# A batched 64x64 matrix product on one Trainium2 core: the preparation of the next tile is put ahead of this tile's matmuls, and b is cast on another engine

## The chip, the cores and the metric

The kernel runs on 1 core of a Trainium2 chip. The time is the device time in microseconds (us) of one execution. A profile of one execution stands beside the times; its span runs from the first to the last instruction of the program, and that execution's own time is a little longer than its span. The engines are called as in the profile: PE is TensorE (PEld its weight loads), DVE is VectorE, ACT is ScalarE, POOL is GpSimd and SP is SyncE. POOL and SP here mostly issue DMAs.

## The reference

1024 independent products of 64x64 matrices, float32 in and out:

```
a: (1024, 64, 64) float32, b: (1024, 64, 64) float32
out = np.matmul(a, b).astype(np.float32)
```

a and b are 16.78 MB each, and so is the output.

## The kernel before

The batch is cut into 16 tiles of 64 products. A tile is 16 groups (g) of 4 products (h). For each tile t:

- **Load.** Four DMAs on POOL's queue (one for each h, L59) bring a into `a_sb`, each 256 KB of float32 that the DMA turns into 128 KB of bfloat16. One DMA on SP's queue (L63) brings 1 MB of b into `b_sb`, as float32. There are four buffers of each, and the loop calls `load(t + 3)` at the head of round t. POOL's DMAs use eight completion semaphores in turn, so a DMA on POOL's queue is not issued before the DMA eight places earlier has landed; a load also waits until the copy out of the buffer that it takes (L80 for a, L103 for b) is done.
- **Prepare.** DVE copies a into `a_bf` (L80), so that the four products of a group stand side by side. PE transposes it in 16 pieces of 128x128 into two PSUM tiles `at_ps` (L88). DVE and ACT copy one half each of every `at_ps` to `at_sb` (L95, L97; for each `at_ps` ACT's copy waits for DVE's). DVE then writes four diagonal blocks of 32 partitions into `at_bd` (L101): the weights of a matmul that does four products at once. The rest of `at_bd` was zeroed at the start (L70); there are two such buffers. DVE also casts b to bfloat16, into `b_bf` (L103).
- **Multiply.** 64 matmuls of 128x128 weights by 128x64 (L111), in four quarters of 16 that go to a PSUM tile `o_ps` each. ACT copies each quarter to `o_sb` (L120); there are three `o_sb` buffers, so the first of these copies for tile t also waits until the store of tile t-3 has landed.
- **Store.** One DMA of 1 MB on POOL's queue (L122), behind the loads of a that were put there earlier.

Each engine works through a fixed list. The list is not in the order of the Python text: when the program is built, a scheduler orders the instructions of each engine, and it has put the 16 tiles in pairs (both tiles are prepared, then both are multiplied, then both are stored). In the names below the number behind `a_sb`, `at_sb` or `o_sb` tells the tiles apart.

Of the kernel before, what the change touches and what calls it, by code (L numbers as in the profile page):

```python
# [1 line left out]

# [5 lines left out]

fp32 = mybir.dt.float32
bf16 = mybir.dt.bfloat16  # L10


@with_exitstack
def kernel(
    ctx: ExitStack,
    tc: tile.TileContext,
    a: bass.AP,
    b: bass.AP,
    out: bass.AP,
):  # L20

    nc = tc.nc
    B, M, K = a.shape
    _, _, N = b.shape
    assert (M, K, N) == (64, 64, 64) and B % 64 == 0

    T = 64
    n_t = B // T
    AHEAD = 3

    a_v = a.rearrange("(t g h) (mp v) k -> t h g mp (v k)", h=4, g=16, v=8)
    b_v = b.rearrange("(t g h) (kp u) n -> t (h kp) g (u n)", h=4, g=16, u=2)
    o_v = out.rearrange("(t g h) (mo w) n -> t (h mo) g (w n)", h=4, g=16, w=2)

    consts = ctx.enter_context(tc.tile_pool(name="consts", bufs=1))
    a_pool = ctx.enter_context(tc.tile_pool(name="a_pool", bufs=AHEAD + 1))  # L40
    b_pool = ctx.enter_context(tc.tile_pool(name="b_pool", bufs=AHEAD + 1))
    work = ctx.enter_context(tc.tile_pool(name="work", bufs=2))
    o_pool = ctx.enter_context(tc.tile_pool(name="o_pool", bufs=3))
    t_psum = ctx.enter_context(
        tc.tile_pool(name="t_psum", bufs=4, space=bass.MemoryType.PSUM)
    )
    o_psum = ctx.enter_context(
        tc.tile_pool(name="o_psum", bufs=4, space=bass.MemoryType.PSUM)
    )

    bd_tiles = [
        consts.tile([128, 64, 4, 32], bf16, name=f"at_bd{i}") for i in range(2)
    ]
    a_tiles, b_tiles = {}, {}

    def load(t):
        a_sb = a_pool.tile([128, 4, 8, 64], bf16, name="a_sb")
        for h in range(4):
            nc.gpsimd.dma_start(  # L59
                out=a_sb[:, h, :, :].rearrange("p v k -> p (v k)"), in_=a_v[t, h]  # L60
            )
        b_sb = b_pool.tile([128, 16, 128], fp32, name="b_sb")
        nc.sync.dma_start(out=b_sb[:], in_=b_v[t])  # L63
        a_tiles[t], b_tiles[t] = a_sb, b_sb

    load(0)
    identity = consts.tile([128, 128], bf16)
    make_identity(nc, identity)
    for bd in bd_tiles:
        nc.vector.memset(bd[:], 0.0)  # L70
    for t in range(1, AHEAD):
        load(t)

    for t in range(n_t):
        if t + AHEAD < n_t:
            load(t + AHEAD)
        a_sb, b_sb, at_bd = a_tiles.pop(t), b_tiles.pop(t), bd_tiles[t % 2]

        a_bf = work.tile([128, 8, 4, 64], bf16, name="a_bf")
        nc.vector.tensor_copy(a_bf[:], a_sb[:].rearrange("p h v k -> p v h k"))  # L80
        a_cols = a_bf[:].rearrange("p v h k -> p v (h k)")

        at_sb = work.tile([128, 2, 2, 128, 4], bf16, name="at_sb")
        for w in range(2):
            at_ps = t_psum.tile([128, 4, 2, 128], bf16, name="at_ps")
            for vo in range(4):
                for u in range(2):
                    nc.tensor.transpose(  # L88
                        at_ps[:, vo, u, :], a_cols[:, 2 * vo + w, u::2], identity[:]
                    )  # L90
            for u in range(2):
                dst = at_sb[:, w, u, :, :]
                src = at_ps[:, :, u, :].rearrange("p vo q -> p q vo")
                if u == 0:
                    nc.vector.tensor_copy(dst, src)  # L95
                else:
                    nc.scalar.copy(dst, src)  # L97
        at_v = at_sb[:].rearrange("p w u (g mp) vo -> p (w u g) (mp vo)", g=16)
        for h in range(4):
            rows = slice(32 * h, 32 * h + 32)  # L100
            nc.vector.tensor_copy(at_bd[rows, :, h, :], at_v[rows, :, :])  # L101
        b_bf = work.tile([128, 16, 128], bf16, name="b_bf")
        nc.vector.tensor_copy(b_bf[:], b_sb[:])  # L103
        o_sb = o_pool.tile([128, 4, 4, 2, 64], fp32, name="o_sb")
        for gq in range(4):
            o_ps = o_psum.tile([128, 4, 2, 64], fp32, name="o_ps")
            for g4 in range(4):
                g = 4 * gq + g4
                for w in range(2):
                    for u in range(2):  # L110
                        nc.tensor.matmul(  # L111
                            o_ps[:, g4, w, :],
                            at_bd[:, (2 * w + u) * 16 + g, :, :].rearrange(
                                "p h mo -> p (h mo)"
                            ),
                            b_bf[:, g, 64 * u : 64 * u + 64],
                            start=(u == 0),
                            stop=(u == 1),
                        )
            nc.scalar.copy(o_sb[:, gq, :, :, :], o_ps[:])  # L120

        nc.gpsimd.dma_start(  # L122
            out=o_v[t], in_=o_sb[:].rearrange("p q g w n -> p (q g w n)")
        )


# [1 line left out]
_INS = ['a', 'b']  # L128
_OUTS = [((1024, 64, 64), 'float32')]


# [23 lines left out]
```

## Time and profile before

| | us |
|---|---|
| median of 3 runs | 151.15 (151.05 to 152.82) |
| the profiled execution's own time | 150.8 |
| its span | 148.9 |

| engine | busy us | share of the span |
|---|---|---|
| PE | 64.4 | 43% |
| DVE | 104.9 | 70% |
| ACT | 53.5 | 36% |
| POOL (mostly issuing DMAs) | 62.6 | 42% |

A share of busy time is a mean over the whole span. The span has a stretch in which loads, work and stores run side by side and a tail in which only work and stores are left, and the two have to be read apart. A row of the timeline gives the start, the duration, the engine, the line and the operation, and in brackets how long the engine had been idle and what ended that. "Landing" is the time from the issue of a DMA until its completion is seen. In the view by stretches of time, the row of each stretch ends with the clock that PE was granted (1.00 is full speed), the mean busy share of the 16 DMA engines (a little over 1 where packets overlap) and the GB/s that they moved; of a this counts the bfloat16 side, half of what is read.

### The profile page before, as it was taken

The numbers are of one execution on the slowest core, as the hardware profiler recorded it, in microseconds if no ns is written. First come the engines' busy times: TensorE is split into PE (matmuls) and PEld (weight loads), VectorE is DVE, ScalarE is ACT, GpSimd is POOL, SyncE is SP. The second block draws the span as 40 slices with busy tenths as digits, with TensorE's granted clock in tenths as the row PEclk, the third lists the DMA queues.
The fourth block names the chain that finished last, engine by engine and source line by source line (L and its number), as shares of the span: only waits on it lengthen the run. The fifth ranks groups of instructions, "written<-read, shape, count | busy, mean of one in ns | idle before, by whom it ended". The sixth has DMA issues, their size and how long they took to land.

```text
span 148.9 us, 3081 instructions
## 1 busy us (share of the span) xinstructions
PE 64.4 (43%) x1280; PEld 62.0 (42%) x1280; DVE 104.9 (70%) x130; ACT 53.5 (36%) x97; POOL 62.6 (42%) x86
## 2 busy tenths in 40 slices
PE   0005225960893058500990079402990059429400
PEld 0004215950893058500890078302880059429400
DVE  5754499799978297938995498919985497994000
ACT  3000052763320914064502733082602827616500
POOL 7644364336622165712983174614754303300410
PEclk9999999998569758955598557965599556975865
DMA  3999999999999999999999999999999995892594
GB/s 77 292 290 292 291 293 293 295 286 276 293 364 383 322 291 275 370 308 290 283 348 366 309 292 287 368 310 291 294 321 369 195 356 207 237 273 68 169 265 129
DMA packets 22031, 42.15 MB, mean 283 GB/s; under 512 B 1537, under 2 KB 9729, under 8 KB 22017
## 3 DMA queue, kind: packets, MB, share of 16 engines
q0 software_dynamic: 13568, 25.17, 66.7%
q1 hardware_dynamic: 8448, 16.78, 33.2%
q8 instruction: 10, 0.16, 0.4%
q14 instruction: 5, 0.03, 0.1%
HBM read 33.55 MB, written 16.78 MB: 338 GB/s over the span
## 4 chain that ended last, share of the span: by engine, by line
DMA 52%; issue 19%; POOL 11%; DVE 5%; PE 4%; ACT 3%; POOLq 1%; ACTq 0%; DVEq 0%
DMA a_sb<-in_a_dram 44%; POOL out_dram L122 8%; DMA out_dram<-o_sb 8%; PE o_ps L111 4%; POOL a_sb L59 2%; DVE at_sb L95 2%; DVE at_bd L101 2%; ACT at_sb L97 2%; ACT o_sb L120 1%; POOLq L150 1%; DVE b_bf L103 1%; DVE a_bf L80 0%; POOL identity masks.py:199 0%; POOL identity masks.py:197 0%; POOLq L122 0%
## 5 line engine op out<-in xcount | busy, mean ns | idle before, releaser
L111 PE MATMUL o_ps<-b_bf,at_bd 128*128 128x64 bf16 x1024 | 48.1, 225 | 59.3 <-DVE at_bd L101 59.3
L111 PEld LDWEIGHTS <-at_bd 128*128 128x128 bf16 x1024 | 46.6, 120 | 61.3 <-DVE at_bd L101 61.3
L59 POOL DMA_DIRECT2D a_sb<-in_a_dram x64 | 41.4, 652 | 50.8 <-DMA a_sb<-in_a_dram 23.7
L101 DVE COPY at_bd<-at_sb 32x2048 bf16<-32x2048 bf16 x64 | 49.7, 776 | 17.5 <-ACT at_sb L97 16.6
L120 ACT COPY o_sb<-o_ps 128x512 f32<-128x512 f32 x64 | 35.6, 591 | 65.7 <-PE o_ps L111 33.5
L122 POOL DMA_DIRECT2D out_dram<-o_sb x16 | 20.6, 1290 | 28.2 <-ACT o_sb L120 21.9
L97 ACT COPY at_sb<-at_ps 128x512 bf16<-128x512 bf16 x32 | 17.4, 624 | 20.2 <-DVE at_sb L95 20.0
L88 PE MATMUL at_ps<-identity,a_bf 128*128 128x128 bf16 x256 | 17.4, 231 | 15.8 <-DVE a_bf L80 15.8
L88 PEld LDWEIGHTS <-a_bf 128*128 128x128 bf16 x256 | 15.9, 104 | 16.1 <-DVE a_bf L80 16.1
L103 DVE CAST b_bf<-b_sb 128x2048 bf16<-128x2048 f32 x16 | 19.3, 1226 | 2.2 <-PE o_ps L111 2.2
L95 DVE COPY at_sb<-at_ps 128x512 bf16<-128x512 bf16 x32 | 19.9, 680 | 0.0
L80 DVE COPY a_bf<-a_sb 128x2048 bf16<-128x2048 bf16 x16 | 10.8, 694 | 8.7 <-DMA a_sb<-in_a_dram 7.7
L70 DVE MEMSET at_bd<- 128x4096 uint32 x2 | 6.9, 3472 | 2.5 <-PEq L139 1.7
L97 ACT ACT_TABLE_LOAD x1 | 1.3, 1283 | 0.7 <-PEq L139 0.7
masks.py:199 POOL TENSOR_SCALAR_AFFINE_SELECT identity<-identity 128x128 bf16<-128x128 bf16 x1 | 0.4, 364 | 0.0
masks.py:197 POOL MEMSET identity<- 128x128 bf16 x1 | 0.3, 266 | 0.0
L139 POOL MEMSET const-float32-0.0<- 128x1 f32 x1 | 0.1, 98 | 0.2 <-issue 0.2
L139 POOL MEMSET const-bfloat16-1.0<- 128x1 bf16 x1 | 0.1, 101 | 0.0
L139 POOL MEMSET const-uint8-127<- 128x1 uint8 x1 | 0.1, 101 | 0.0
L139 POOL MEMSET const-float32-1.0<- 128x1 f32 x1 | 0.1, 98 | 0.0
## 6 DMA issues: line engine op xcount, KB each, us to landing
out_dram<-o_sb POOLq DMA_DIRECT2D x16, 1024.0 KB, 10.9
a_sb<-in_a_dram POOLq DMA_DIRECT2D x64, 128.0 KB, 11.7
b_sb<-in_b_dram SPq DMA_DIRECT2D x16, 0.5 KB, 14.8
```

The source lines that it names most:

```text
L59: nc.gpsimd.dma_start(out=a_sb[:, h, :, :].rearrange("p v k -> p (v k)"), in_=a_v[t, h])
L70: nc.vector.memset(bd[:], 0.0)
L80: nc.vector.tensor_copy(a_bf[:], a_sb[:].rearrange("p h v k -> p v h k"))
L88: nc.tensor.transpose(at_ps[:, vo, u, :], a_cols[:, 2 * vo + w, u::2], identity[:])
L95: nc.vector.tensor_copy(dst, src)
L97: nc.scalar.copy(dst, src)
L101: nc.vector.tensor_copy(at_bd[rows, :, h, :], at_v[rows, :, :])
L103: nc.vector.tensor_copy(b_bf[:], b_sb[:])
L111: nc.tensor.matmul(o_ps[:, g4, w, :], at_bd[:, (2 * w + u) * 16 + g, :, :].rearrange("p h mo -> p (h mo)"), b_bf[:, g, 64 * u : 64 * u + 6 ...
L120: nc.scalar.copy(o_sb[:, gq, :, :, :], o_ps[:])
L122: nc.gpsimd.dma_start(out=o_v[t], in_=o_sb[:].rearrange("p q g w n -> p (q g w n)"))
L150: with _tile.TileContext(nc) as tc:
```

## The change

The body of the loop is split into `prepare(t)` and `multiply(t)`. `prepare(0)` stands ahead of the loop, and round t calls `load(t + 4)`, then `prepare(t + 1)`, then `multiply(t)`. Beside that:

- loads are called four tiles ahead instead of three, with the same four buffers;
- there are three `at_bd` buffers instead of two, and so three memsets at the start;
- the cast of b goes from DVE to ACT, between the copies to `at_sb` and those of the diagonal blocks;
- of the last tile, DVE copies the second and the fourth quarter to `o_sb`, ACT the first and the third, and each quarter is stored by a DMA of its own (256 KB) as soon as it is copied.

```
-    AHEAD = 3
+    AHEAD = 4
...
-    a_pool = ctx.enter_context(tc.tile_pool(name="a_pool", bufs=AHEAD + 1))
-    b_pool = ctx.enter_context(tc.tile_pool(name="b_pool", bufs=AHEAD + 1))
+    a_pool = ctx.enter_context(tc.tile_pool(name="a_pool", bufs=AHEAD))
+    b_pool = ctx.enter_context(tc.tile_pool(name="b_pool", bufs=AHEAD))
...
+    N_BD = 3
     bd_tiles = [
-        consts.tile([128, 64, 4, 32], bf16, name=f"at_bd{i}") for i in range(2)
+        consts.tile([128, 64, 4, 32], bf16, name=f"at_bd{i}") for i in range(N_BD)
     ]
...
+    def prepare(t):
+        a_sb, b_sb, at_bd = a_tiles.pop(t), b_tiles.pop(t), bd_tiles[t % N_BD]
...
+        b_bf = work.tile([128, 16, 128], bf16, name="b_bf")
+        nc.scalar.copy(b_bf[:], b_sb[:])
+        bf_tiles[t] = b_bf
...
-        b_bf = work.tile([128, 16, 128], bf16, name="b_bf")
-        nc.vector.tensor_copy(b_bf[:], b_sb[:])
+
+    def multiply(t):
+        at_bd, b_bf = bd_tiles[t % N_BD], bf_tiles.pop(t)
+        last = t == n_t - 1
...
-            nc.scalar.copy(o_sb[:, gq, :, :, :], o_ps[:])
+            if last and gq % 2:
+                nc.vector.tensor_copy(o_sb[:, gq, :, :, :], o_ps[:])
+            else:
+                nc.scalar.copy(o_sb[:, gq, :, :, :], o_ps[:])
+            if last:
+                nc.gpsimd.dma_start(
+                    out=o_v[t, :, 4 * gq : 4 * gq + 4, :],
+                    in_=o_sb[:, gq, :, :, :].rearrange("p g w n -> p (g w n)"),
+                )
+        if not last:
+            nc.gpsimd.dma_start(
+                out=o_v[t], in_=o_sb[:].rearrange("p q g w n -> p (q g w n)")
+            )
...
+    prepare(0)
+    for t in range(n_t):
+        if t + AHEAD < n_t:
+            load(t + AHEAD)
+        if t + 1 < n_t:
+            prepare(t + 1)
+        multiply(t)
```

The scheduler orders the new text anew. Three places show what it makes of it; tiles 0 to 15 are counted in the order of the program.

DVE, the end of its list, before: `a_bf_1667` and `a_bf_1772` belong to tiles 14 and 15, and so do `at_sb_1669` and `at_sb_1774`.

```order
L101 COPY at_bd0_76<-at_sb_1459 32x64x32 x4
L101 COPY at_bd1_77<-at_sb_1564 32x64x32 x4
L80 COPY a_bf_1667<-a_sb_1338 128x2048
L80 COPY a_bf_1772<-a_sb_1450 128x2048
L103 CAST b_bf_1696<-b_sb_1343 128x2048
L103 CAST b_bf_1801<-b_sb_1455 128x2048
L95 COPY at_sb_1669<-at_ps_1670 128x512
L95 COPY at_sb_1669<-at_ps_1681 128x512
L95 COPY at_sb_1774<-at_ps_1775 128x512
L95 COPY at_sb_1774<-at_ps_1786 128x512
L101 COPY at_bd0_76<-at_sb_1669 32x64x32 x4
L101 COPY at_bd1_77<-at_sb_1774 32x64x32 x4
```

DVE, the end of its list, now: `at_sb_1492`, `at_sb_1597` and `at_sb_1702` belong to tiles 13, 14 and 15, `a_bf_1595` and `a_bf_1700` to tiles 14 and 15.

```order
L85 COPY at_sb_1492<-at_ps_1504 128x512
L70 COPY a_bf_1595<-a_sb_1266 128x2048
L94 COPY at_bd1_77<-at_sb_1492 32x64x32 x4
L85 COPY at_sb_1597<-at_ps_1598 128x512
L85 COPY at_sb_1597<-at_ps_1609 128x512
L70 COPY a_bf_1700<-a_sb_1378 128x2048
L94 COPY at_bd2_78<-at_sb_1597 32x64x32 x4
L85 COPY at_sb_1702<-at_ps_1703 128x512
L85 COPY at_sb_1702<-at_ps_1714 128x512
L94 COPY at_bd0_76<-at_sb_1702 32x64x32 x4
L116 COPY o_sb_1805<-o_ps_1825 128x512
L116 COPY o_sb_1805<-o_ps_1863 128x512
```

The pairs are gone, the casts are gone, and the diagonal blocks of a tile now stand behind the copy of the next tile's a, which waits for that tile's load.

ACT, near the end of its list, before: the copies to `at_sb` of tiles 14 and 15, then the quarters of tile 14 (`o_sb_1698`) and tile 15.

```order
L120 COPY o_sb_1593<-o_ps_1648 128x512
L97 COPY at_sb_1669<-at_ps_1670 128x512
L97 COPY at_sb_1669<-at_ps_1681 128x512
L97 COPY at_sb_1774<-at_ps_1775 128x512
L97 COPY at_sb_1774<-at_ps_1786 128x512
L120 COPY o_sb_1698<-o_ps_1699 128x512
L120 COPY o_sb_1698<-o_ps_1717 128x512
```

ACT, the same place now: `o_sb_1626` is tile 13, `b_bf_1725` and `at_sb_1702` are tile 15, `o_sb_1731` is tile 14.

```order
L118 COPY o_sb_1626<-o_ps_1645 128x512
L118 COPY o_sb_1626<-o_ps_1663 128x512
L118 COPY o_sb_1626<-o_ps_1681 128x512
L89 CAST b_bf_1725<-b_sb_1383 128x2048
L87 COPY at_sb_1702<-at_ps_1703 128x512
L87 COPY at_sb_1702<-at_ps_1714 128x512
L118 COPY o_sb_1731<-o_ps_1732 128x512
L118 COPY o_sb_1731<-o_ps_1750 128x512
```

The cast of b stands between the quarters of one tile and the copies to `at_sb` two tiles further on, and these stand ahead of the next tile's quarters.

POOL, the end of its list, before: `a_sb_1338` and `a_sb_1450` are the a of tiles 14 and 15, `o_sb_1040` and `o_sb_1152` are the stores of tiles 8 and 9, `o_sb_1264` that of tile 10.

```order
L122 DMA out_0_dram<-o_sb_1040 128x16x128
L122 DMA out_0_dram<-o_sb_1152 128x16x128
L59 DMA a_sb_1338<-in_a_dram 128x1x512
L59 DMA a_sb_1450<-in_a_dram 128x1x512 x4
L122 DMA out_0_dram<-o_sb_1264 128x16x128
L122 DMA out_0_dram<-o_sb_1376 128x16x128
```

POOL, the end of its list, now: `a_sb_1266` and `a_sb_1378` are tiles 14 and 15, `o_sb_1192`, `o_sb_1304` and `o_sb_1416` are the stores of tiles 9, 10 and 11, `o_sb_1805` that of tile 15.

```order
L125 DMA out_0_dram<-o_sb_1192 128x16x128
L60 DMA a_sb_1266<-in_a_dram 128x1x512 x4
L125 DMA out_0_dram<-o_sb_1304 128x16x128
L60 DMA a_sb_1378<-in_a_dram 128x1x512 x4
L125 DMA out_0_dram<-o_sb_1416 128x16x128
L125 DMA out_0_dram<-o_sb_1521 128x16x128
L125 DMA out_0_dram<-o_sb_1626 128x16x128
L125 DMA out_0_dram<-o_sb_1731 128x16x128
L120 DMA out_0_dram<-o_sb_1805 128x4x128 x4
```

The stores stand singly among the loads, and one store more (that of tile 10) stands ahead of the last loads of a.

More of the change, by code (lines that the diff above doesn't have):

```diff
@@ L49 @@
     )
+    N_BD = 3
     bd_tiles = [
-        consts.tile([128, 64, 4, 32], bf16, name=f"at_bd{i}") for i in range(2)
+        consts.tile([128, 64, 4, 32], bf16, name=f"at_bd{i}") for i in range(N_BD)
     ]
-    a_tiles, b_tiles = {}, {}
+    a_tiles, b_tiles, bf_tiles = {}, {}, {}
     def load(t):
@@ L64, in load @@
         a_tiles[t], b_tiles[t] = a_sb, b_sb
[L66 to L77, printed above, removed]
+    def prepare(t):
+        a_sb, b_sb, at_bd = a_tiles.pop(t), b_tiles.pop(t), bd_tiles[t % N_BD]
         a_bf = work.tile([128, 8, 4, 64], bf16, name="a_bf")
@@ L119 @@
                         )
[L120 to L124, printed above, removed]
+            if last and gq % 2:
[11 more added lines that the diff above has]
+            )
+    load(0)
+    identity = consts.tile([128, 128], bf16)
+    make_identity(nc, identity)
+    for bd in bd_tiles:
+        nc.vector.memset(bd[:], 0.0)
+    for t in range(1, AHEAD):
+        load(t)
+    prepare(0)
[5 more added lines that the diff above has]
+        multiply(t)
 _INS = ['a', 'b']
```

## The prediction

> **What bounds the kernel now.** I read the page first: who is busy, and what the DMA engines do over the span.
>
> ```profile
> PE 64.4 (43%) x1280; PEld 62.0 (42%) x1280; DVE 104.9 (70%) x130; ACT 53.5 (36%) x97; POOL 62.6 (42%) x86
> DMA  3999999999999999999999999999999995892594
> HBM read 33.55 MB, written 16.78 MB: 338 GB/s over the span
> ```
>
> No compute engine is full, while the DMA engines are, from the second slice of 3.7 us to the 33rd; then gaps begin. So there are two stretches, and I looked at each by itself. First the full one, with the first matmuls of two pairs of tiles, three pairs apart, and one row of the view by stretches:
>
> ```profile
> 53.98 3.35 PE L111 MATMUL o_ps<-b_bf,at_bd 128*128 128x64 bf16 x64 [7.95 <-DVE at_bd L101]
> 103.23 3.60 PE L111 MATMUL o_ps<-b_bf,at_bd 128*128 128x64 bf16 x64 [8.61 <-DVE at_bd L101]
> 87.00:103.20 16.20, 7.29 (x158) 6.96 (x155) 12.33 (x16) 6.36 (x12) 7.79 (x11) 0.71 1.09 313
> ```
>
> A pair takes (103.23 - 53.98)/3 = 16.4 us, 8.2 us for a tile. A pair moves 2 x 3 x 1.05 = 6.29 MB at the HBM, so 383 GB/s, with the DMA share at 1.09. PE, DVE and ACT have idle time in that row, PE before L111 above all, but nothing that an engine does faster there moves the end: the transfers set the pace. All 50.33 MB at 383 GB/s are 131 us. With 2.6 us at the start (the first digit is 3: 0.7 of 3.7 us idle) and the 1.9 us after the last transfer (below), a span of about 136 us would be the floor; 148.9 is 13 above it. That is lost in the tail:
>
> ```profile
> 112.09 0.51 POOL L59 DMA_DIRECT2D a_sb<-in_a_dram  x1 [0.57 <-DMA a_sb<-in_a_dram]
> DMA to landing us min/median/max: 9.8/9.8/9.8
> 123.42 1.30 DVE L80 COPY a_bf<-a_sb 128x2048 bf16<-128x2048 bf16 x2
> 130.16 5.58 DVE L101 COPY at_bd<-at_sb 32x2048 bf16<-32x2048 bf16 x8
> 132.98 6.54 PE L111 MATMUL o_ps<-b_bf,at_bd 128*128 128x64 bf16 x128 [4.61 <-DVE at_bd L101]
> 135.76 0.59 ACT L120 COPY o_sb<-o_ps 128x512 f32<-128x512 f32 x1 [0.27 <-PE o_ps L111]
> 137.49 1.15 POOL L122 DMA_DIRECT2D out_dram<-o_sb  x1 [8.79 <-ACT o_sb L120]
> 140.71 1.15 POOL L122 DMA_DIRECT2D out_dram<-o_sb  x1 [2.06 <-ACT o_sb L120]
> ...
> 122.40:125.00 2.60, 2.60 (x53) 2.60 (x51) 2.56 (x5) 1.76 (x3) 0.00 (x0) 0.50 0.83 307
> 125.00:127.00 2.00, 2.00 (x61) 2.00 (x59) 1.23 (x2) 1.84 (x4) 1.46 (x1) 0.96 0.24 86
> 127.00:135.00 8.00, 3.39 (x63) 3.21 (x61) 7.90 (x12) 3.19 (x7) 1.15 (x1) 0.81 0.93 262
> 135.00:139.00 4.00, 4.00 (x82) 4.00 (x80) 0.72 (x2) 2.84 (x5) 1.15 (x1) 0.52 0.02 6
> 139.00:147.00 8.00, 0.52 (x18) 0.40 (x14) 0.00 (x0) 1.07 (x2) 1.15 (x1) 0.70 0.91 262
> 147.00:148.90 1.90, 0.00 (x0) 0.00 (x0) 0.00 (x0) 0.00 (x0) 0.00 (x0) 0.50 0.00 0
> ```
>
> The last load of a is issued at 112.09 and lands 9.8 later, at 121.9; I call that moment T. From T to the end 27.0 us pass. DVE is still at the blocks of tiles 12 and 13 and takes up the last pair only at 123.42; both tiles of it are prepared before the first is multiplied, at 132.98. Meanwhile the DMA engines idle: (1 - 0.83) x 2.6 + (1 - 0.24) x 2 + (1 - 0.93) x 8 + (1 - 0.02) x 4 + (1 - 0.91) x 8 = 7.1 us, plus 1.9 us at the close. And the stores of the tail run slower than the backlog did:
>
> ```profile
> 111.00:113.00 2.00, 0.40 (x8) 0.23 (x5) 2.00 (x4) 0.00 (x0) 1.38 (x3) 1.00 1.02 385
> 144.00:146.00 2.00, 0.00 (x0) 0.00 (x0) 0.00 (x0) 0.00 (x0) 0.00 (x0) 0.50 1.00 289
> ```
>
> At 111 to 113, stores and some last loads in a full queue move 385 GB/s; at 144 to 146 a store by itself moves 289 with the engines as busy. So a store of 1.05 MB costs 2.7 us out of a backlog and 3.6 us in the tail.
>
> **The change, part by part.** The durations that it moves, and the waits:
>
> ```profile
> L101 DVE COPY at_bd<-at_sb 32x2048 bf16<-32x2048 bf16 x64 | 49.7, 776 | 17.5 <-ACT at_sb L97 16.6
> L120 ACT COPY o_sb<-o_ps 128x512 f32<-128x512 f32 x64 | 35.6, 591 | 65.7 <-PE o_ps L111 33.5 <-DMA out_dram<-o_sb 32.1
> L97 ACT COPY at_sb<-at_ps 128x512 bf16<-128x512 bf16 x32 | 17.4, 624 | 20.2 <-DVE at_sb L95 20.0
> L103 DVE CAST b_bf<-b_sb 128x2048 bf16<-128x2048 f32 x16 | 19.3, 1226 | 2.2 <-PE o_ps L111 2.2
> L95 DVE COPY at_sb<-at_ps 128x512 bf16<-128x512 bf16 x32 | 19.9, 680 | 0.0
> L80 DVE COPY a_bf<-a_sb 128x2048 bf16<-128x2048 bf16 x16 | 10.8, 694 | 8.7 <-DMA a_sb<-in_a_dram 7.7 <-issue 0.7
> L70 DVE MEMSET at_bd<- 128x4096 uint32 x2 | 6.9, 3472 | 2.5 <-PEq L139 1.7 <-issue 0.8
> ACT o_sb L120 <- DMA out_dram<-o_sb: 32.1, 5, 7.0
> ```
>
> *The cast of b on ACT.* No row shows it. Below, it can't cost less than the same engine's copy of a quarter of the elements, 0.59 us; above, four such copies, 2.36. I take 2.0, near the upper end, since four times the elements pass through. DVE loses 1.23 us a tile and needs 0.69 + 2 x 0.68 + 4 x 0.78 = 5.2; ACT now needs 2.0 + 2 x 0.62 + 4 x 0.59 = 5.6. Both stay under the 8.2 us that the transfers of a tile take, so in the full stretch the cast costs nothing; if that cover goes, ACT is the slowest engine. Two casts (tiles 14 and 15) stand on ACT's list in the tail and count there.
>
> The Trainium skill, page "ScalarE: Activation LUTs", section "What ACT_TABLE_LOAD costs", gives 186 ns plus 0.833 ns per element, an estimate of 1.9 us here; the sum below would end 0.1 to 0.2 us earlier by it. The same page's rules for kernel authors speak against the move, since they put plain arithmetic on VectorE; the row above, 1.23 us for the cast on DVE, bears that out, and no row of before shows the other side.
>
> *SP's queue.* A load of b now waits for ACT's cast instead of DVE's.
>
> ```profile
> SPq L63 <- DVE b_bf L103: 50.0, 11, 12.0
> 94.98 4.18 SPq L63 DMA_DIRECT2D b_sb<-in_b_dram  x1
> ```
>
> SP waits 50 us for casts as it is, and its last load goes out at 94.98, 27 us ahead of T. A cast that comes some us later costs nothing as long as POOL's queue keeps the DMA engines full.
>
> *POOL's queue.* The stores now stand singly, each behind the first loads of tile t+5 or behind all of t+4, and each waits for the DMA eight places back and for ACT. At a store, up to seven other DMAs (2 MB or more, 5 us) are still in flight, and ACT must only have got through tile t, while the queue itself is some two tiles further; so I see no starving, and cost it at 0. Bounds: a gain is excluded, since the share is already at 1; a loss of one whole store's 2.7 us is what it could be if POOL once ran dry.
>
> *The third memset* (3.47 us, L70) stands ahead of the first copy of a on DVE.
>
> ```profile
> 11.38 0.69 DVE L80 COPY a_bf<-a_sb 128x2048 bf16<-128x2048 bf16 x1 [1.97 <-DMA a_sb<-in_a_dram]
> 18.78 1.87 POOL L59 DMA_DIRECT2D a_sb<-in_a_dram  x2 [0.99 <-DVE at_sb L95]
> ```
>
> DVE had 1.97 us idle there; the copy slips from 11.4 to about 13.7. The first load that needs its buffer goes out at 18.78, because POOL's queue gets there only then. Cost 0.
>
> *T itself.* The stretch up to T is full before and after. What has been moved by T: all loads and the stores that stand ahead of the last ones. Before, up to 122.4 that was 50.33 - 5.2 = 45.1 MB, the 5.2 being the rows from 122.40 on (GB/s times length: 0.80 + 0.17 + 2.10 + 0.02 + 2.10), so loads and 11.0 stores. Now the stores of tiles 0 to 10 stand ahead, 11 too. T stays at 121.9.
>
> *The tail,* from T. Near the end the b loads are through, and a tile of a and a store alternate: 2.1 MB at 385 is 5.5 us from one a to the next, and ACT needs 5.6 a tile, so I give DVE and ACT about 1.5 us of backlog. DVE: the copy of a for tile 15, then the blocks of 14, 0.7 each as in the row at 130.16 (5.58/8): 0.7 + 2.8 + 1.5 = T+5. Tile 14's matmuls start there, 6 us earlier than before (132.98 is T+11.1, with two tiles prepared); they take 4 x (0.59 + 0.27) = 3.4 us, as in the row at 135.76, at the clock of 0.50. DVE copies `at_sb` of 15 until T+6.4; ACT has tile 13's quarters and the cast of 15 ahead of its half, and ends it at about T+7.9. From there two things run: DVE's blocks of 15 until T+10.7, matmuls until T+14.1; and ACT's four quarters of 14 (4 x 0.59) until T+10.3, when its store is issued. Before, that store was issued at 137.49, T+15.6.
>
> The transfers: stores 11 and 12 are ready and run from T to T+5.4 at 2.7 each. Store 13 needs tile 13's quarters, T+5; a store moved 1.7 us after its issue (137.49 to about 139.2), so it runs from T+6.7 to T+10.3 at 3.6. Store 14 is issued at T+10.3, runs from T+12 to T+15.6. The four parts of 15 are issued between T+12 and T+15, the last in time, and take 3.6 us together: T+19.2. With the close of 1.9 that is T+21.1. The split itself gains little, since store 14 is still in the queue when the parts come; without it the one store would be issued at T+14.8, 0.8 us ahead of its turn with 1.7 us to start, so 0.9 us at most.
>
> Sum: 27.0 - 21.1 = 5.9 us. Span 121.9 + 21.1 = 143.0, the execution 150.8 - 5.9 = 144.9. The median of the runs is 0.35 over the profiled execution, so 145.2.
>
> **The rivals.**
>
> - *The tail packs tighter.* ACT and DVE have kept up and stores 11 to 15 all come out of a backlog: 5 x 2.7 + 1.7 + 1.9 = T+17.1, a time of 141.2. For: tiles can be worked on one at a time. Against: tile 14's blocks still wait behind tile 15's load. Chance 0.14.
> - *The tail is as long as before,* 150 to 151, anything from 148.1 up. The static lists put blocks behind the next tile's load and ACT's quarters behind the next tile's halves; with the cast at its upper end ACT needs 6.0 us against 5.5, and if ACT is a tile (5.6 us) behind at T, the gain is gone. Against: up to T it has 8.2 us a tile for most of the way. This is also the case in which the change does nothing, since waits of PE for blocks (the largest in the trace) never set the pace. Chance 0.21.
> - *Slower: single stores run at the slow rate throughout.* The pairs of stores in POOL's list may be what made the fast rate, one behind the other; stores of the tail, single, ran at 289. If the 11 stores ahead of T each cost 3.6 instead of 2.7, T is 10 us later, and the time 155. It decides from about 9 of the 11. Against: the 385 were seen with one store of tile 10 among loads, and the loads fill the queue behind each store now. Chance 0.07.
>
> **How the numbers follow.** A measurement of this kernel can tell about 2% from no change, so faster means under 148.1 and slower over 154.2. The forecast has the rest, 0.58, with a range of its own of 142.5 to 148: 1.5 us of backlog gone or doubled, 2.7 us for a dry queue. Faster is 0.58 + 0.14 = 0.72, the same 0.21, slower 0.07. The 8-in-10 range must take in the tight tail and half of the third case: 140.5 to 151.
>
> **What would show it.** The DMA row full until about 122 and the last landing of a there; the execution's idle DMA time in the tail under 4 us instead of 7.1; tile 14's matmuls at about T+5; a cast row on ACT near 2.0 us, and DVE's busy time near 104.9 - 19.6 + 3.5 = 89. If the last load of a lands after 125, the part on the full stretch is wrong; if it lands at 122 and the end still comes after 147, the part on ACT's list is.

## The result, and the profile after

The changed kernel takes 143.96 us (median of 4 runs, 143.01 to 144.35) against 151.1 us before: a ratio of 0.950, 95% interval 0.941 to 0.959. The forecast was 145.2 us. The profiled execution took 144.35 us, with a span of 142.6. (Runs of a kernel that lie over 1.5% above its fastest are left out of its ratio; for one kernel below, the two stages alone, only one run is then left, and it has no interval.)

The page of the kernel after, in the same rows as before:

```profile
PE 69.4 (49%) x1280; PEld 65.3 (46%) x1280; DVE 89.9 (63%) x117; ACT 79.2 (56%) x111; POOL 60.9 (43%) x89
DMA  3999999999999999999999999999999999975892
HBM read 33.55 MB, written 16.78 MB: 353 GB/s over the span
L89 ACT CAST b_bf<-b_sb 128x2048 bf16<-128x2048 f32 x16 | 30.8, 1926 | 9.4 <-DMA b_sb<-in_b_dram 9.4
```

The same bytes moved in 6.3 us less. The digits of the DMA row are full for 35 slices of 3.57 us, to 124.8, where before it was 33 slices of 3.72, to 122.8; what is shorter is the part behind that. The timeline and the view by stretches of the kernel after, for that part:

```profile
113.36 0.51 POOL L60 DMA_DIRECT2D a_sb<-in_a_dram  x1 [0.91 <-DMA a_sb<-in_a_dram]
DMA to landing us min/median/max: 8.9/8.9/8.9
122.40 0.69 DVE L70 COPY a_bf<-a_sb 128x2048 bf16<-128x2048 bf16 x1 [0.76 <-DMA a_sb<-in_a_dram]
124.51 1.34 POOL L125 DMA_DIRECT2D out_dram<-o_sb  x1 [5.38 <-ACT o_sb L118]
126.40 2.04 PE L106 MATMUL o_ps<-b_bf,at_bd 128*128 128x64 bf16 x64 [1.51 <-DVE at_bd L94]
130.53 1.32 POOL L125 DMA_DIRECT2D out_dram<-o_sb  x1 [4.68 <-ACT o_sb L118]
131.15 3.54 PE L106 MATMUL o_ps<-b_bf,at_bd 128*128 128x64 bf16 x64 [2.71 <-DVE at_bd L94]
135.71 0.75 POOL L120 DMA_DIRECT2D out_dram<-o_sb  x1 [0.21 <-issue]
...
87.00:103.20 16.20, 6.54 (x90) 5.85 (x88) 9.20 (x15) 9.19 (x16) 5.58 (x8) 0.50 1.09 329
122.30:125.00 2.70, 2.58 (x39) 2.41 (x36) 2.57 (x4) 2.70 (x5) 0.49 (x1) 0.61 1.03 357
125.00:127.00 2.00, 0.60 (x21) 0.61 (x22) 1.96 (x4) 1.00 (x1) 0.85 (x1) 1.00 0.62 207
129.00:131.00 2.00, 0.00 (x0) 0.00 (x0) 1.97 (x3) 1.24 (x3) 0.47 (x1) 1.00 0.56 166
131.00:133.00 2.00, 1.85 (x36) 1.86 (x37) 0.09 (x1) 0.58 (x1) 0.85 (x1) 0.56 0.26 78
133.00:140.20 7.20, 1.69 (x32) 1.52 (x29) 1.38 (x2) 0.58 (x1) 3.01 (x4) 0.74 0.96 269
140.20:142.60 2.40, 0.00 (x0) 0.00 (x0) 0.00 (x0) 0.00 (x0) 0.00 (x0) 0.50 0.03 10
```

The last a lands at 113.36 + 8.9 = 122.3 us (121.9 before), and the span ends 20.3 us later (27.0 before). DVE is there in time for it: it had waited 0.76 us when it took up tile 15 at 122.40, where before it came to the last pair 1.5 us late. The matmuls of tile 14 start at 126.40, 4.1 us behind the landing instead of 11.1, and its store is issued at 130.53, 8.2 us behind it instead of 15.6. In the tail the DMA engines idle for 0.38 x 2 + 0.44 x 2 + 0.74 x 2 + 0.04 x 7.2 = 3.4 us, where it was 7.1.

### The profile page after: what moved, and what is told of

The parts are those of the page before. It is cut to its first block, busy times and chain, and to the rows that moved or that the text cites. A ratio compares the mean times of both kernels' runs of the same rounds, so it can differ in the third digit from the quotient of the medians.

```text
span 142.6 us, 3074 instructions
## 1 busy us (share of the span) xinstructions
PE 69.4 (49%) x1280; PEld 65.3 (46%) x1280; DVE 89.9 (63%) x117; ACT 79.2 (56%) x111; POOL 60.9 (43%) x89
## 4 chain that ended last, share of the span: by engine, by line
DMA 66%; issue 13%; POOL 8%; ACT 4%; DVE 3%; POOLq 1%; DVEq 0%; ACTq 0%
DMA a_sb<-in_a_dram 48%; DMA out_dram<-o_sb 18%; POOL out_dram L125 4%; POOL a_sb L60 2%; DVE at_bd L94 2%; POOL out_dram L120 2%; ACT at_sb L87 2%; ACT o_sb L118 1%; ACT b_bf L89 1%; DVE at_sb L85 1%; POOLq L168 1%; DVE a_bf L70 1%; POOL identity masks.py:199 0%; POOL identity masks.py:197 0%; POOLq L125 0%
## 5 line engine op out<-in xcount | busy, mean ns | idle before, releaser
L106 PEld LDWEIGHTS <-at_bd 128*128 128x128 bf16 x1024 | 45.1, 117 | 27.6 <-DVE at_bd L94 27.1
L60 POOL DMA_DIRECT2D a_sb<-in_a_dram x64 | 38.4, 606 | 40.6 <-DMA a_sb<-in_a_dram 22.8
L94 DVE COPY at_bd<-at_sb 32x2048 bf16<-32x2048 bf16 x64 | 47.7, 745 | 4.5 <-ACT at_sb L87 3.6
L78 PE MATMUL at_ps<-identity,a_bf 128*128 128x128 bf16 x256 | 23.7, 268 | 40.1 <-DVE a_bf L70 40.1
L118 ACT COPY o_sb<-o_ps 128x512 f32<-128x512 f32 x62 | 32.9, 603 | 12.7 <-DMA out_dram<-o_sb 8.1
L78 PEld LDWEIGHTS <-a_bf 128*128 128x128 bf16 x256 | 20.7, 123 | 41.6 <-DVE a_bf L70 41.6
L89 ACT CAST b_bf<-b_sb 128x2048 bf16<-128x2048 f32 x16 | 30.8, 1926 | 9.4 <-DMA b_sb<-in_b_dram 9.4
L125 POOL DMA_DIRECT2D out_dram<-o_sb x15 | 19.1, 1271 | 33.1 <-ACT o_sb L118 15.0
L85 DVE COPY at_sb<-at_ps 128x512 bf16<-128x512 bf16 x32 | 20.3, 684 | 0.7 <-PE at_ps L78 0.5
L133 DVE MEMSET at_bd<- 128x4096 uint32 x3 | 10.4, 3472 | 3.3 <-PEq L157 1.7
L120 POOL DMA_DIRECT2D out_dram<-o_sb x4 | 3.0, 754 | 1.6 <-ACT o_sb L118 1.2
L116 DVE COPY o_sb<-o_ps 128x512 f32<-128x512 f32 x2 | 1.4, 692 | 2.9 <-PE o_ps L106 2.9
## 6 DMA issues: line engine op xcount, KB each, us to landing
a_sb<-in_a_dram POOLq DMA_DIRECT2D x64, 128.0 KB, 11.1
```

The lines of the kernel that those rows point to most:

```text
L60: nc.gpsimd.dma_start(out=a_sb[:, h, :, :].rearrange("p v k -> p (v k)"), in_=a_v[t, h])
L78: nc.tensor.transpose(at_ps[:, vo, u, :], a_cols[:, 2 * vo + w, u::2], identity[:])
L89: nc.scalar.copy(b_bf[:], b_sb[:])
L106: nc.tensor.matmul(o_ps[:, g4, w, :], at_bd[:, (2 * w + u) * 16 + g, :, :].rearrange("p h mo -> p (h mo)"), b_bf[:, g, 64 * u : 64 * u + 6 ...
L120: nc.gpsimd.dma_start(out=o_v[t, :, 4 * gq : 4 * gq + 4, :], in_=o_sb[:, gq, :, :, :].rearrange("p g w n -> p (g w n)"),)
L125: nc.gpsimd.dma_start(out=o_v[t], in_=o_sb[:].rearrange("p q g w n -> p (q g w n)"))
```

## The experiments

My theory was that until the last a has landed the transfers set the pace, and that the gain lies behind that landing. The runs had to tell whether that is so, and which part of the change brought the end of the tail forward. The kernel before was run beside every group of four, with medians of 150.9 to 151.1 us.

### Each part of the change by itself

**The two stages alone.** The changed kernel with the cast on DVE and the last tile stored whole:

```
-        nc.scalar.copy(b_bf[:], b_sb[:])
+        nc.vector.tensor_copy(b_bf[:], b_sb[:])
...
-            if last and gq % 2:
-                nc.vector.tensor_copy(o_sb[:, gq, :, :, :], o_ps[:])
-            else:
-                nc.scalar.copy(o_sb[:, gq, :, :, :], o_ps[:])
...
+            nc.scalar.copy(o_sb[:, gq, :, :, :], o_ps[:])
...
```

> The changed kernel with the cast of b back on DVE and the last tile stored whole: the two stages, three block buffers and loads four ahead are all that is left of the change. Theory of the tail (loads set the pace until the last a lands at about 122 us, the gain is what no longer idles after that): the cast on DVE costs 1.2 us of DVE time behind that moment and takes 1.9 us off ACT, so the time is 144 to 146 us, the last landing of a again at 122 plus or minus 1.5. Rival (DVE's relief by 1.2 us a tile is what helped): DVE is as loaded as before, 149 to 151 us. Rival (the four parts of the last store helped): 146.5 us or more.

Measured: 152.17 us, the median of 7 runs, six of them from 151.9 to 152.9 and one at 149.67, without a ratio. By the six it is 1 us slower than before, by the one 1.4 us faster. Either way most of the gain is missing: my theory had put the time at 144 to 146 us. The run at 149.67 lies where the rival had it (149 to 151: DVE's relief from the casts is what helped). The last a lands at 118.9, earlier than the 122 plus or minus 1.5 that I had given.

**The last tile stored whole.** The changed kernel without the four parts:

```
-            if last:
-                nc.gpsimd.dma_start(
-                    out=o_v[t, :, 4 * gq : 4 * gq + 4, :],
-                    in_=o_sb[:, gq, :, :, :].rearrange("p g w n -> p (g w n)"),
-                )
-        if not last:
-            nc.gpsimd.dma_start(
-                out=o_v[t], in_=o_sb[:].rearrange("p q g w n -> p (q g w n)")
-            )
+        nc.gpsimd.dma_start(
+            out=o_v[t], in_=o_sb[:].rearrange("p q g w n -> p (q g w n)")
+        )
```

> The changed kernel with the last tile stored by one DMA, all four quarters copied by ACT. Theory of the tail: the store of tile 14 is still being moved when the parts come, so the parts save at most about 0.9 us: 144 to 145 us. Rival (the parts matter, since the last store waits for its last quarter and then starts from nothing): 146.5 us or more.

Measured: 143.07 us, a ratio of 0.948 (0.942 to 0.955) to the kernel before, against 0.950 with the parts. It is a little under the 144 to 145 us that I had given. The parts bring nothing that can be measured. (DVE's two copies of quarters go with them.)

**The cast alone.** The kernel before with one line changed:

```
-        nc.vector.tensor_copy(b_bf[:], b_sb[:])
+        nc.scalar.copy(b_bf[:], b_sb[:])
```

> The kernel before with only the cast of b moved to ACT; the program then also comes out in another order, with the blocks of the tiles of a pair no longer side by side. Theory of the tail: until the last a lands nothing changes (122 plus or minus 1.5 us); what counts is how early tile 14 is multiplied behind that, and the new order allows it earlier than 11 us behind, so 144 to 149 us. Rival (the two stages in the text are needed): 150 to 152 us, no change.

Measured: 152.39 us, a ratio of 1.008 (1.004 to 1.011): slightly slower, outside what I had given for the theory and for the rival. So the cast gains nothing alone, the two stages 1% at best, and both together 5%.

**The four parts alone,** with DVE's two copies of quarters, in the kernel before:

```
+        last = t == n_t - 1
...
+            if last:
+                nc.gpsimd.dma_start(
+                    out=o_v[t, :, 4 * gq : 4 * gq + 4, :],
+                    in_=o_sb[:, gq, :, :, :].rearrange("p g w n -> p (g w n)"),
+                )
...
```

> The kernel before with only the last tile stored in four parts, the second and fourth quarters copied by DVE. Theory of the tail: the transfers of the last two stores run without a gap from 139 to 147 us already, so the parts cannot end earlier: 150 to 151 us. Rival (the parts are worth something by themselves): the last store is 1.15 us of issue and its start behind the last quarter, 148.5 us or less.

Measured: 150.72 us, a ratio of 0.997 (0.994 to 1.001). As expected.

In all four the last a lands at 118.9 to 122.0 us, so none of them loses its time ahead of that. It is the tail that differs, and the trace of the two stages alone shows a reason why it is long there (the trace is of the run at 152.9 us; of the run at 149.67 there is none). Its timeline, tiles 11 and 12:

```profile
112.97 0.58 ACT L115 COPY o_sb<-o_ps 128x512 f32<-128x512 f32 x1 [3.63 <-DMA out_dram<-o_sb]
113.45 0.59 ACT L87 COPY at_sb<-at_ps 128x512 bf16<-128x512 bf16 x1
114.08 3.40 DVE L94 COPY at_bd<-at_sb 32x2048 bf16<-32x2048 bf16 x4 [3.55 <-ACT at_sb L87]
117.54 3.59 PE L106 MATMUL o_ps<-b_bf,at_bd 128*128 128x64 bf16 x64 [7.49 <-DVE at_bd L94]
```

ACT waits 3.63 us to copy a quarter, because the output buffer is still being stored; the next copy to `at_sb` stands behind it; DVE's blocks wait 3.55 us for that copy, and PE waits 7.49 us for the blocks. The same chain is in the kernel before, at tiles 11 to 13:

```profile
114.47 2.05 ACT L120 COPY o_sb<-o_ps 128x512 f32<-128x512 f32 x4 [7.02 <-DMA out_dram<-o_sb]
117.54 5.85 DVE L101 COPY at_bd<-at_sb 32x2048 bf16<-32x2048 bf16 x8 [3.75 <-ACT at_sb L97]
120.63 5.95 PE L111 MATMUL o_ps<-b_bf,at_bd 128*128 128x64 bf16 x128 [9.23 <-DVE at_bd L101]
```

The waits of the kernel before, of the kernel before with the cast on ACT, and of the kernel after, in that order (us in total, how many, the longest):

```profile
ACT o_sb L120 <- DMA out_dram<-o_sb: 32.1, 5, 7.0
DVE at_bd L101 <- ACT at_sb L97: 16.6, 5, 3.8
```

```profile
ACT o_sb L120 <- DMA out_dram<-o_sb: 24.3, 5, 9.5
DVE at_bd L101 <- ACT at_sb L97: 20.7, 8, 7.8
```

```profile
ACT o_sb L118 <- DMA out_dram<-o_sb: 8.1, 4, 3.5
DVE at_bd L94 <- ACT at_sb L87: 3.6, 4, 2.1
```

So a second theory: with three output buffers the preparation of a tile is held up by the store of an older one, by way of ACT's list, and the changed kernel escapes this, since its stores go out earlier and ACT's list has the copies to `at_sb` ahead of the quarters.

### The waits for an output buffer taken away

Six output buffers instead of three take ACT's wait away (2.4 us of it stay in the two stages alone) without touching anything else: the list of every engine stays as it was.

```
-    o_pool = ctx.enter_context(tc.tile_pool(name="o_pool", bufs=3))
+    o_pool = ctx.enter_context(tc.tile_pool(name="o_pool", bufs=6))
```

In the kernel before:

> The kernel before with six output buffers instead of three; the list of every engine is the same, only ACT's copies no longer wait for an older store to land (32.1 us in five waits). Theory of the waits (ACT, held at a store, holds the copies to at_sb behind it, and DVE's blocks with them): the last pair is taken up at the landing of the last a, some 122 us, instead of 123.4, and its first matmul comes at about 131 instead of 133; the stores of tiles 12 and 13 come out of the backlog. 148.5 to 149.8 us, since the pair still waits for tile 15. If the waits are all of the lag: 146 us or less. If they are nothing: 151.

Measured: 149.3 us, 0.989 (0.983 to 0.994), as expected.

In the two stages alone:

> The two stages alone (cast on DVE, last tile stored whole) with six output buffers instead of three, every engine's list unchanged. Its tail was 32 us long with the last a landing at 118.9. Theory of the waits: ACT's waits for stores (22.7 us) held the preparation of the next tile, and without them it falls to 144 to 147 us. Rival (DVE's load: 6.4 us a tile against 5.5 us from one a to the next at the end): DVE stays late, 149 us or more.

Measured: 148.2 us, 0.981 (0.977 to 0.985), with the last landing at 118.9, as with three buffers. That is 4.0 us less by the medians, but 1.5 against the one run at 149.67, and 2.0 by the fastest runs (149.67 and 147.64). So these waits were 1.5 to 4 us of its lag; the rest stays, and the time lies between what the two theories gave.

In the kernel before with the cast on ACT:

> The kernel before with the cast on ACT and six output buffers instead of three, lists unchanged against the same with three. Theory of the waits: ACT waited 24.3 us for stores; without that the blocks of tiles 13 and 14 come earlier, 146 to 149 us. Rival (the order of the lists, with tile 15 taken up only behind the blocks of two tiles): 151 us or more, as with three buffers (152.4).

Measured: 145.84 us, 0.966 (0.962 to 0.969): 6.5 us less than with three buffers. It is more than I had given, and the other order of the lists is no obstacle.

In the changed kernel:

> The changed kernel with six output buffers instead of three, lists unchanged. ACT's waits for stores are 8.1 us there and lie in the full stretch. Theory: nothing to gain, 143 to 144.5 us, a landing of the last a at about 122. Rival (the waits still cost in the tail): 141.5 us or less.

Measured: 143.28 us, 0.952 (0.945 to 0.959), the last landing at 121.3. The changed kernel has nothing to gain from more buffers, as expected.

Free of these waits the four kernels stand in a row that can be read: 149.3 for the kernel before, 148.2 with the two stages, 145.8 with the cast on ACT, 143.3 with both (and the parts, which are worth nothing). The cast is the larger half, 3.5 us by itself and 4.9 on top of the two stages; the stages are 1.1 by themselves, with intervals that overlap, and 2.6 on top of the cast.

### What the cast does

The two kernels with the two stages and six buffers, with the cast on DVE and then on ACT, take up tile 15 like this:

```profile
122.39 0.68 DVE L70 COPY a_bf<-a_sb 128x2048 bf16<-128x2048 bf16 x1
121.52 0.69 DVE L70 COPY a_bf<-a_sb 128x2048 bf16<-128x2048 bf16 x1 [0.17 <-DMA a_sb<-in_a_dram]
```

With the cast on DVE the last a lands at 118.9 and DVE comes to it 3.5 us late; it was busy for 18.1 of the 18.4 us from 104.7 to 123.1. With the cast on ACT it was busy for 15.1 of the same 18.4 us and waited for the landing, at 121.3. So in this order of the lists the casts are what puts DVE behind.

In the order of before the casts also stand behind the last landing. When all casts move, the scheduler also orders the lists anew. To tell the two effects apart, only the casts of the last two tiles were moved, in the kernel before with six buffers; the rest of the lists stays in pairs.

```
+        if t >= 14:
+            nc.scalar.copy(b_bf[:], b_sb[:])
+        else:
+            nc.vector.tensor_copy(b_bf[:], b_sb[:])
```

> The kernel before with six output buffers, and the cast of b on ACT for tiles 14 and 15 alone. Apart from these two casts the lists are those of before, in pairs. It separates the two ways in which the cast on ACT can help. If it is DVE's time behind the last landing (two casts, 2.4 us, ahead of the last pair's blocks): 146.6 to 147.6 us against 149.3. If it is the other order that the lists take when all casts move: 149 us, no change.

Measured: 147.04 us, 0.978 (0.974 to 0.981), which is 2.3 us less than with six buffers alone by the medians and 1.6 by the ratios (0.989 - 0.978 of 151). The timelines of the kernel before with six buffers, and then of this one, show where:

```profile
122.44 0.69 DVE L80 COPY a_bf<-a_sb 128x2048 bf16<-128x2048 bf16 x1 [0.77 <-DMA a_sb<-in_a_dram]
123.05 3.00 DVE L103 CAST b_bf<-b_sb 128x2048 bf16<-128x2048 f32 x2
125.97 2.47 DVE L95 COPY at_sb<-at_ps 128x512 bf16<-128x512 bf16 x4
131.19 5.11 PE L111 MATMUL o_ps<-b_bf,at_bd 128*128 128x64 bf16 x128 [4.86 <-DVE at_bd L101]
```

```profile
122.32 0.93 DVE L80 COPY a_bf<-a_sb 128x2048 bf16<-128x2048 bf16 x1 [1.74 <-DMA a_sb<-in_a_dram]
123.98 2.49 DVE L95 COPY at_sb<-at_ps 128x512 bf16<-128x512 bf16 x4 [0.73 <-PE at_ps L88]
129.21 5.45 PE L114 MATMUL o_ps<-b_bf,at_bd 128*128 128x64 bf16 x128 [3.93 <-DVE at_bd L101]
```

Both take up tile 15 when it lands. In the first, two casts (3.00 us) stand between that and the copies to `at_sb`; in the second they don't, and the first matmul of the last pair comes 2.0 us earlier. So 1.6 to 2.3 of the 3.5 us can be had from DVE's time behind the last landing alone. The rest comes with the casts of the other tiles and the order of the lists; that was not taken apart further. With all casts on ACT and six buffers, the last a lands at 120.1, 2.3 us earlier than in the kernel before with six buffers (122.4), and the tail behind it is as long (24.3 and 24.5 us).

### Whether the transfers set the pace up to the last landing

The changed kernel with six buffers, with 4.2 MB of the output left out. Tiles 2 to 9 are stored by half only. The loads and the work on the engines are as before, but the scheduler has put some entries of the lists of POOL, DVE, ACT and PE in another order:

```
+            nq = 2 if 2 <= t < 10 else 4
             nc.gpsimd.dma_start(
-                out=o_v[t], in_=o_sb[:].rearrange("p q g w n -> p (q g w n)")
+                out=o_v[t, :, : 4 * nq, :],
+                in_=o_sb[:, :nq, :, :, :].rearrange("p q g w n -> p (q g w n)"),
```

> The changed kernel with six output buffers, which for tiles 2 to 9 stores only the first half of the output (so 4.2 MB less are written); all loads and all work on the engines are as before. Theory (until the last a lands, the transfers set the pace): 4.19 MB at 383 GB/s are 10.9 us, the last a lands at about 111 instead of 122, and the time is 131.5 to 134 us. Rival (the engines and their waits set the pace of the full stretch): the last landing stays at 118 or later and the time at 139 us or more.

Measured: 135.71 us, 0.899 (0.892 to 0.907); the last a lands at 107.0. The landing moved by more than I gave, and the time by less. The rows of this kernel's timeline:

```profile
100.26 0.52 POOL L60 DMA_DIRECT2D a_sb<-in_a_dram  x1 [0.15 <-issue]
DMA to landing us min/median/max: 6.7/6.7/6.7
113.10 1.23 DVE L70 COPY a_bf<-a_sb 128x2048 bf16<-128x2048 bf16 x1
```

In the list of POOL the store of tile 10 had slipped behind the last loads, and that of tile 9 too, so what stands ahead of them is two whole stores and seven halves, 5.8 MB, where the changed kernel has eleven stores, 11.5 MB. At 383 GB/s the 5.8 MB of difference are 15.1 us, and the landing moved by 121.3 - 107.0 = 14.3 us. So the moment of the last landing follows the bytes that stand ahead of it. And the engines are not far behind: DVE had waited for tile 14 until 103.15, worked from there without a gap, and took up tile 15 only at 113.10, 6 us after it had landed; the tail is 27.2 us long. The copy of tile 15 stands behind the blocks of two tiles here (12 and 13), which is part of the other order. That DVE becomes the bound with fewer bytes is shown for this list alone.

### A faster tail

The stores of tiles 14 and 15 in four parts each, in the changed kernel with six buffers; first all on POOL's queue, then every second one on SP's:

```
-            if last:
-                nc.gpsimd.dma_start(
+            if t >= 14:
+                (nc.sync if gq % 2 else nc.gpsimd).dma_start(
...
-        if not last:
+        if t < 14:
```

> The changed kernel with six output buffers, and the stores of both last tiles in four parts each on POOL's queue (the changed kernel has that for tile 15 alone); the other lists are unchanged. Theory: the first part of tile 14 can go about 1.8 us ahead of the whole store, so the transfers of the last two tiles begin earlier: 141.3 to 142.5 us. Rival (what runs behind the last landing is bound by ACT and PE, not by the start of the store): 143 us, as without it. The rate of the last transfers should stay near 287 GB/s.

Measured: 142.85 us, 0.949 (0.947 to 0.951), no gain over 143.28 that can be told, and more than the 141.3 to 142.5 us that I had given.

> As the stores in four parts for tiles 14 and 15, but every second part goes out on SP's queue, which has nothing left to load. It tells why the late stores move at 287 GB/s and not at 385. If a single queue's ring is the limit, the last stretch reaches 350 GB/s or more and the time is 139.5 to 141.5 us. If it is the memory or the write itself, the rate stays at 287 and the time is that of the parts on POOL alone, 141.3 to 142.5.

Measured: 141.86 us, 0.942 (0.938 to 0.946). This is the fastest of those that store everything, 1.4 us under the changed kernel with six buffers, though not by what I had set out to test. The rate of its stores:

```profile
122.00:124.00 2.00, 2.00 (x42) 2.00 (x40) 1.97 (x4) 1.93 (x4) 0.00 (x0) 0.50 1.03 387
134.00:136.00 2.00, 0.00 (x0) 0.00 (x0) 0.00 (x0) 0.00 (x0) 0.00 (x0) 1.00 1.02 270
136.00:138.00 2.00, 0.00 (x0) 0.00 (x0) 0.00 (x0) 0.00 (x0) 0.00 (x0) 0.51 0.94 277
```

With two queues the last stores move at 270 to 277 GB/s, not at 350 or more, so a single queue's ring is not what slows them. The gain over the parts on POOL may lie in the time of issue: four parts on POOL took 3.28 us to issue (from 128.69), while here POOL had two and SP the others. This was not measured by itself.

## Why the prediction was right, and where it was not

**The stretch up to the last landing: right, in part by luck.** I put T at 121.9 because as many bytes stand ahead of the last load as before; it was 122.3. Over thirteen kernels with all the bytes it was 118.9 to 122.4, and with 5.8 MB fewer ahead it was 107.0. But more had been moved by then than I said. The views from the last landing to the end, before and after:

```profile
121.90:148.90 27.00, 13.01 (x268) 12.71 (x265) 12.90 (x19) 11.09 (x20) 4.92 (x4) 0.69 0.66 199
122.30:142.60 20.30, 8.16 (x167) 7.71 (x164) 9.31 (x13) 7.96 (x13) 5.67 (x6) 0.75 0.72 218
```

Before, 27.0 us at 199 GB/s are 5.4 MB that were left; after, 20.3 at 218 are 4.4 MB, so the tail had 4.2 stores to move where I had five. The stretch up to T moved about 0.9 MB more in 0.4 us more: 50.33 MB less what was left, over T, are 369 GB/s before and 375 after. What made it denser is not shown, and neither is what it was worth in the tail. The third memset, SP's queue and POOL's single stores cost nothing that can be seen there, as said.

**The tail: right in sum.** T+21.1 was given and T+20.3 measured; idle DMA time under 4 us was given and 3.4 measured. Step by step, behind T:

| | predicted | measured |
|---|---|---|
| first matmul of tile 14 | 5.0 | 4.1 |
| store of tile 14 issued | 10.3 | 8.2 |
| first matmul of tile 15 | 10.7 | 8.9 |
| end of the span | 21.1 | 20.3 |

The term that was mis-sized is the backlog of 1.5 us: DVE and ACT had none, and both had waited just before (DVE 0.76 us for tile 15). Against that, the four blocks of tile 14 took 3.33 us, where 2.8 had been given. Of the 2.1 us by which the store of 14 came early only 0.8 reached the end. From 133 on the transfers ran at 269 GB/s with a share of 0.96 (289 had been worked with), and the close took 2.4 us, not 1.9.

**Why there was no backlog: wrong.** In the step on the cast I put the move to ACT at nothing up to T and saw it only as a load on ACT's list in the tail. By the runs it is the larger half of the gain. In the order of before, two casts on DVE stood between the last landing and the last blocks, and taking them away was worth 1.6 to 2.3 us; with the two stages, the casts put DVE 3.5 us behind when the last a landed. My steps for the tail had no cast on DVE, so the sum had this gain in it, but I put it down to tile 14 being prepared by itself: I had the row (123.42, both tiles prepared before the first matmul) and didn't count the two casts of 1.23 us behind it as something that the change takes off that path. With the cast left on DVE the same argument gave 144 to 146 us, and 148.2 came out even with six output buffers. The price of the cast itself was near: 2.0 us given, 1.93 measured. The Trainium skill's "ScalarE: Activation LUTs", section "What ACT_TABLE_LOAD costs", has 186 ns plus 0.833 ns per element, an estimate of 1.9 us here. This trace agrees. The Trainium skill's "ScalarE: Activation LUTs", section "Rules for kernel authors", puts relu, max, min, add and mul on VectorE; a cast is not on that list, and read for one the rule would have kept it where it was. On DVE the row is 1.23 us, 0.7 faster, and yet the kernel gains by the slower place, since DVE was the engine that the tail waited for.

**The waits for output buffers: not seen as a cause.** I quoted ACT's 32.1 us of waits for stores, and used them for nothing. They explain why DVE was still at the blocks of tiles 12 and 13 when the last a landed (1.6 us of the time, by the run with six buffers). They are also much of why each half of the change alone comes to little or nothing: 152.2 us (149.67 in one run) and 152.4 with three buffers, 148.2 and 145.8 with six. I took the change for a sum of parts, and with three buffers it isn't one. That the changed kernel itself is free of them (8.1 us, none of it in the tail) was luck in my argument.

**The rivals.** The tail packed tighter, by compute that kept up: half of it came, the compute kept up, but the stores did not come out of the backlog, since those of 13 to 15 moved at the slow rate. The tail as long as before: no; the two stages without the cast on ACT come near it. Single stores at the slow rate throughout: no. At 122 to 124 the stores of tiles 11 and 12, issued singly, moved at 387 GB/s in the run with two queues, whose POOL list is the same up to there.

**The four parts:** at most 0.9 us was given, nothing could be measured.

## What to carry to other kernels

Where the transfers are full up to the last load, look for the gain behind the moment when it lands, and list everything that each engine still has to do from there to the last store; an instruction that costs nothing in the middle of the kernel can cost most of its length there (here 2.5 us of casts, worth 1.6 to 2.3), and moving it to a slower engine that is idle can pay. An engine that works through a fixed list passes a wait for an output buffer on to whatever stands behind it, here the preparation of the next tile, so count the output buffers before judging an order. And when a change has two parts, measure each alone and together: a wait that neither removes can hide both.

## What was not expected of the hardware

With the DMA engines equally busy, stores move at two rates. At 122 to 124 the stores of tiles 10 to 12 moved at 354 to 387 GB/s (shares of 0.96 to 1.04) in all the kernels that have POOL's list as before or as in the changed kernel, also where the last load had landed already. The stores behind them moved at some 250 to 295 (1.02 and 270 at 134 to 136, above). Two queues instead of one don't change that, nor do parts of 256 KB. That the fast ones were issued while loads were still in flight is not what makes the difference. In the kernel before with the cast on ACT and six buffers, three stores are issued from 114.25 on, ahead of the last landing at 120.1, and they move at the slow rate behind it:

```profile
114.25 3.64 POOL L122 DMA_DIRECT2D out_dram<-o_sb  x3
121.00:124.00 3.00, 3.00 (x61) 3.00 (x59) 2.25 (x4) 2.20 (x5) 0.00 (x0) 0.50 1.00 264
```

So the rule that the prediction worked with, 2.7 us for a store out of a backlog and 3.6 for one in the tail, held for the changed kernel and does not hold for this one. What makes the difference stays open. At these rates each of the three late stores of the changed kernel cost about 1 us more.
